# A two-layer token mixer on one core: projections between the score blocks by issue edges, attention weights of the merge in one load

## The chip, the cores and the metric

The kernel runs as one program on one core of a Trainium2 chip. What counts is the device time of one execution in microseconds, as the median over several runs. A NeuronCore has a matmul engine (TensorE, "PE" in the profile, with its weight loads as "PEld"), VectorE ("DVE"), ScalarE ("ACT"), GpSimd ("POOL", unused here) and the queue engine SyncE ("SP"), which issues all large DMAs of this kernel in order.

## The reference, cut to what matters

The model is a two-layer block over 256 context and 256 latent tokens of width 1024. Each layer has a half-step SwiGLU feed-forward network, then three token mixers side by side on one normalised input, then another feed-forward half step. The change is in the mixers and in their merge:

```python
u, gq, gk, gv, nq, nk, nv, gates = split_in(h @ w_in)       # latent; the same of hc for the context
y_ssm = s5_mixer(u, ...)                                     # width 384, with a GLU behind it
y_gqa = window_gqa_latent(rope(gq), rope(gk), gv, ...)       # 8 heads, 2 key/value heads
y_na  = neighborhood_attn_latent(nq, nk, nv, ..., rpb)       # 8 heads
m = sigmoid(g_s) * (y_ssm @ w_p_ssm) + sigmoid(g_a) * (y_gqa @ w_p_gqa) + sigmoid(g_n) * (y_na @ w_p_na)
x = x + ml[5] * (m @ w_out)
```

Latent tokens attend to context and latent, context tokens to the context alone. In the last layer the context has no output, so only its keys, values and recurrence are needed there.

## The kernel before, in words

Activations lie as 128 channels by tokens; columns 0 to 255 are the context, 256 to 511 the latent tokens. Every large product is made of three float32r matmuls (`mm3`): a weight `raw` is loaded by `wload`, ScalarE rounds it to `whi`, VectorE subtracts to get `wlo`, and the product is whi·h + whi·l + wlo·h. `wload` rotates three buffers each of `raw`, `whi` and `wlo` (pool `wp`), and `bank` three PSUM banks.

`mixer(l)` runs once for each layer. `proj(j, a, b)` is one projection of 128 output channels: a load of 512 KB and 24 matmuls of up to 512 columns (256 in layer 1 for what only the latent tokens need, N = 256 there). A loop over `c` handles two head pairs per turn: a GQA attend (heads c and 4 + c) and a neighbourhood attend (NA). Its steps in the order in which they are traced are: GQA queries (`gqa_queries`), one or two gate projections (`fill`), the GQA attend, NA keys and values (`na_keys`), a step of the recurrence (`pump`), NA queries, gates, the NA attend, a step of the recurrence. A gate computed ahead is stored in DRAM (`parked`) and read back in the merge (`gate_back`).

`attend` loops over streams (context and latent; in layer 1 latent alone) and in each over two blocks of 128 queries. A block has four score matmuls into two PSUM banks `sc` (one for each of two heads, hf 0 and 1; there are two such banks), then for each head a softmax on VectorE and ScalarE, transposes on TensorE into `pt` and a copy into `ptb`. A stream ends with `values`, float32 matmuls of 64 weight columns (two passes each) into the two halves of a bank `po`. I write s0b1 for block 1 of the context stream and s1b0 for block 0 of the latent stream.

`put_k` and `put_q` write keys and queries as high and low parts on ScalarE and VectorE; `rotate` applies the rotary angles.

Each engine runs its instructions in the order that is settled when the program is built. The builder goes by what would be ready; among ready instructions of an engine, the one traced first goes first. `tc.issue_after(ins)` queues what is traced inside it, on the engine of `ins`, behind `ins`: an edge of order, not a wait for its end. `pe_anchor[0]` is the last matmul of `mm3` traced so far.

After the loop come three gates (`ths`), the pools of the attention are closed, and the merge opens pool `gp` for `yh` and `yl` (high and low parts of the 11 chunks of y: 3 SSM, 4 GQA, 4 NA) and `mgh`, `mgl`. The SSM output goes through Gelu and the GLU (three banks `pgl`). Then for each of 8 output chunks m the three branches b (SSM 3, GQA 4, NA 4 chunks of k) are multiplied, each with a `wload` of its own weights, gated and added; last the output projection `wout`.

Of the kernel before, what the change touches and what calls it, by code (L numbers as in the profile page):

```python
# [10 lines left out]
F32 = mybir.dt.float32  # L11
# [8 lines left out]
KC = 8  # L20
# [7 lines left out]
def body(tc, A):  # L28
    nc = tc.nc
# [43 lines left out]
    def wload(src, n, pool=None, tag=""):  # L73
        raw = wp.tile([128, 1024], F32, name="raw", tag="raw")
        nc.sync.dma_start(raw[:, :n], src)
        hi = (pool or wp).tile([128, 1024], F32R, name="whi", tag="whi" + tag)
        S.activation(hi[:, :n], raw[:, :n], AF.Copy)  # L77
        lo = (pool or wp).tile([128, 1024], F32R, name="wlo", tag="wlo" + tag)
        anchor[0] = V.tensor_sub(lo[:, :n], raw[:, :n], hi[:, :n].bitcast(F32)).ins  # L79
        return hi, lo  # L80
# [562 lines left out]
    def mixer(l):  # L643
# [89 lines left out]
        def values(nk_, ptb, vt, out):  # L733
            po = pa.tile([128, T], F32, name="po", tag="po")
            for j in range(nk_):
                for hf, r in enumerate(halves):
                    PE.matmul(po[r, :HALF], vt[:, j, r], ptb[hf][:, j], start=j == 0, stop=j == nk_ - 1)  # L737
            S.copy(out, po[:, :HALF])

        def attend(K, Q, vt, out, heads, bias):  # L740

            for s in streams:
                nk_ = 4 if s else 2
                extra = bias() if s else None
                ptb = [ip.tile([128, 4, 2, 128], F32, name="ptb", tag="ptb", bufs=4) for hf in range(2)]
                for b in range(2):
                    q0 = HALF * s + 128 * b
                    ps = [pa.tile([128, T], F32, name="sc", tag="sc", bufs=2) for hf in range(2)]
                    for hf in range(2):
                        for j in range(2):  # L750
                            PE.matmul(ps[hf][:, :128 * nk_], Q[:, hf, q0:q0 + 128], K[:, hf, j, :128 * nk_], start=j == 0, stop=j == 1)  # L751
                    for hf in range(2):
                        if s:
                            k0, n, x = extra(hf, b)
                            V.tensor_add(ps[hf][:, k0:k0 + n], ps[hf][:, k0:k0 + n], x)
                        softmax(ps[hf], nk_, ptb[hf], b, heads[hf], "pt", 1)
                values(nk_, ptb, vt, out[:, HALF * s:HALF * s + HALF])
# [10 lines left out]
        def gqa_queries(c):  # L768
# [5 lines left out]
            return Q  # L774

        def na_keys(c):
            ps = proj(CH_NK + c, 0, T)
            K = stack_k("n")
            put_k(K, slice(0, T), ps)
            return K, v_proj(CH_NV + c, "n")  # L780

# [121 lines left out]
        parked = tc.dram_tile([3 * KC, 128, T], F32, name=f"parked{l}")  # L903
        ahead = [3 * m + b for m in range(1, KC) for b in ((1, 2) if last else (2,))]
        queue = list(ahead)

        def fill():
            for j in queue[:2 if last else 1]:
                queue.remove(j)
                nc.sync.dma_start(parked[j, :, :N], gate(j)[:, :N])  # L910

        def gate_back(j):
            th = mo.tile([128, T], F32, name="th", tag="th", bufs=3)
            nc.sync.dma_start(th[:, :N], parked[j, :, :N])
            return th

        KG = gqa_keys()
        pump()
        for c in range(4):
            Q = gqa_queries(c)  # L920
            fill()
            attend(KG[0], Q, KG[1], gq[:, c], (c, 4 + c), window)
            KN = na_keys(c)
            pump()
            Q = na_queries(c)
            fill()
            attend(KN[0], Q, KN[1], nq[:, c], (None, None), lambda: near(c))
            pump()
        pump(9)
        ths = [gate(j) for j in range(3)]  # L930
        mi.close()

        gp = xs.enter_context(tc.tile_pool(name=f"mg{l}", bufs=1))
        p3 = xs.enter_context(tc.tile_pool(name=f"p3{l}", bufs=3, space=PSUM))
        yh = gp.tile([128, 11, T], F32R, name="yh")
        yl = gp.tile([128, 11, T], F32R, name="yl")
        nat = lambda x: x.rearrange("p (x t) -> p x t", t=8)
# [3 lines left out]
        for c in range(3):  # L941
            split(nat(yh[:, c, c0:]), nat(yl[:, c, c0:]), ty[c])
        pgs = []
        for c in range(3):
            wh, wl = wload(A["wglu"][l, c], 384)
            ps = bank("pgl")
            for k in range(3):
                w = slice(128 * k, 128 * k + 128)
                mm3(ps[:, :N], wh[:, w], wl[:, w], yh[:, k, c0:], yl[:, k, c0:], k == 0, k == 2)
            pgs.append(ps)  # L950
        for c in range(3):
            g = pgs[c][:, :N]
            S.activation(g, g, AF.Tanh, scale=0.5)
            V.scalar_tensor_tensor(ty[c], nat(g), 1.0, ty[c], op0=ALU.add, op1=ALU.mult)
            glu_last = split(nat(yh[:, c, c0:]), nat(yl[:, c, c0:]), ty[c], scale=0.5)
        for src, o in ((gq, 3), (nq, 7)):
            for c in range(4):
                split(yh[:, o + c, c0:], yl[:, o + c, c0:], src[:, c, c0:])
        mh = gp.tile([128, KC, T], F32R, name="mgh")
        ml = gp.tile([128, KC, T], F32R, name="mgl")  # L960
        spans = ((0, 3), (3, 7), (7, 11))
# [15 lines left out]
        for m in range(KC):  # L977
            acc = gp.tile([128, T], F32, name="macc", tag="macc")
            for b, (k0, k1) in enumerate(spans):
                j = 3 * m + b  # L980
                th = ths[b] if m == 0 else gate_back(j) if j in ahead else gate(j)
                wh, wl = wload(A["wp"][l, m][:, 128 * k0:128 * k1], 128 * (k1 - k0))
                pp = p3.tile([128, T], F32, name="pbr", tag="pbr")
                for k in range(k0, k1):
                    w = slice(128 * (k - k0), 128 * (k - k0) + 128)
                    mm3(pp[:, :N], wh[:, w], wl[:, w], yh[:, k, c0:], yl[:, k, c0:], k == k0, k == k1 - 1)
                if b == 0:
                    V.scalar_tensor_tensor(acc[:, :N], th[:, :N], 1.0, pp[:, :N], op0=ALU.add, op1=ALU.mult)
# [3 lines left out]
                if m:  # L992
                    later(0.01 * N + 0.00125 * N * (k1 - k0))
            split(mh[:, m, c0:], ml[:, m, c0:], acc[:, :N])
        later.finish()
# [3 lines left out]
        for s in streams:  # L999
            a, b = HALF * s, HALF * s + HALF  # L1000
            ctx_norm = norm(l, 2, 0, 2) if s and not last else iter(())
            for m in range(KC):
                if m >= 2:
                    next(ctx_norm, None)
                wh, wl = wload(A["wout"][l, m], 1024)
                ps = bank("pwo")
                for k in range(KC):
                    w = slice(128 * k, 128 * k + 128)
                    mm3(ps[:, :HALF], wh[:, w], wl[:, w], mh[:, k, a:b], ml[:, k, a:b], k == 0, k == KC - 1)
                evac_x(m, ps, l, 1, a, b)  # L1010
# [157 lines left out]
```

## Time and profile before

| | |
|---|---|
| median of 3 runs | 2246.77 us (2242.68 to 2249.39) |
| the profiled execution's own time | 2243.03 us |
| span of the profile | 2241.2 us |
| TensorE busy | 2167.7 us, 97% |
| VectorE busy | 1644.6 us, 73% |
| ScalarE busy | 944.7 us, 42% |
| layer 0: attention, merge and output projection from | 484 us, 736 us, 885 us |
| layer 1: the same from | 1736 us, 1930 us, 2005 us |

Times in the profile are microseconds from the span's start. Matmuls overlap: a matmul's duration is longer than its distance to the next, so busy time says little of TensorE's pace. "Idle" before an instruction is the time in which its engine had nothing running, and the name behind the arrow is what ended it.

### The profile page before, as it was taken

How to read it: one execution, taken by the hardware profiler on the slowest of the kernel's cores; microseconds unless marked ns; L12 is line 12 of the kernel's file. 1: busy time of each engine (PE TensorE's matmuls, PEld its weight loads, DVE VectorE, ACT ScalarE, POOL GpSimd, SP SyncE). 2: the span in 40 equal slices, each digit the busy share in tenths (PEclk: the TensorE clock that was granted, in tenths of full speed). 3: DMA queues.
4: the chain of work that ended last, by engine and by line, in shares of the span. 5: the costliest groups of instructions: out<-in, count | busy, mean ns of one | idle time of the engine just before them, and what ended most of it. 6: DMA issues, size and time to landing. Idle time of an engine off the chain costs nothing.

```text
span 2241.2 us, 33869 instructions
## 1 busy us (share of the span) xinstructions
PE 2167.7 (97%) x12842; PEld 1851.8 (83%) x12842; DVE 1644.6 (73%) x3208; ACT 944.7 (42%) x1604; POOL 0.7 (0%) x6
## 2 busy tenths in 40 slices
PE   6999999999999999999999999999999999899997
PEld 3787888987777788988888998888899888798997
DVE  4897887777665888897787797777867776566555
ACT  3322333466566423432222443223245665544443
POOL 0000000000000000000000000000000000000000
PEclk9999999999999999999999999999999999999999
DMA  7635544643431566675565555555556554265554
GB/s 272 210 113 169 198 160 141 224 144 104 137 114 43 176 196 202 207 226 166 183 207 179 165 179 182 162 162 181 179 161 217 160 171 131 70 213 157 172 196 123
DMA packets 141626, 378.16 MB, mean 169 GB/s; under 512 B 30868, under 2 KB 38548, under 8 KB 141464
## 3 DMA queue, kind: packets, MB, share of 16 engines
q1 hardware_dynamic: 140880, 375.88, 52.0%
q8 instruction: 101, 1.65, 0.3%
q14 instruction: 61, 0.50, 0.1%
q10 hardware_dynamic: 584, 0.12, 0.0%
HBM read 346.45 MB, written 29.50 MB: 168 GB/s over the span
## 4 chain that ended last, share of the span: by engine, by line
PE 81%; DVE 9%; ACT 4%; DMA 3%; issue 2%; SPq 0%; ACTq 0%; DVEq 0%
PE pgu L85 11%; PE pgu L83 11%; PE pgu L84 11%; PE pd L85 5%; PE pd L84 5%; PE pd L83 5%; PE pp L83 4%; PE pp L84 4%; PE pp L85 4%; DVE wlo L79 2%; PE po L737 2%; PE pt L729 2%; PE sc L751 2%; ACT whi L77 1%; DMA raw<-dn 1%
## 5 line engine op out<-in xcount | busy, mean ns | idle before, releaser
L77 ACT ACTIVATE whi<-raw 128x1024 fp32r<-128x1024 f32 (+4 forms) x520 | 477.5, 920 | 954.9 <-issue 284.3
L79 DVE TENSOR_TENSOR wlo<-raw,whi 128x1024 fp32r<-128x1024 f32 (+4 forms) x520 | 543.7, 1047 | 281.4 <-ACT whi L77 279.6
L83 PE MATMUL pgu<-Hh,whi 128*128 128x512 f32 (+1 forms) x1360 | 495.1, 365 | 4.2 <-ACT Hh L159 3.0
L85 PE MATMUL pgu<-Hh,wlo 128*128 128x512 f32 (+1 forms) x1360 | 494.7, 364 | 0.9 <-DVE wlo L79 0.9
L84 PE MATMUL pgu<-Hl,whi 128*128 128x512 f32 (+1 forms) x1360 | 494.5, 364 | 0.0
L85 PE MATMUL pd<-mid,wlo 128*128 128x256 f32 (+1 forms) x968 | 305.0, 315 | 2.0 <-DVE wlo L79 2.0
L83 PE MATMUL pd<-mid,whi 128*128 128x256 f32 (+1 forms) x968 | 303.7, 314 | 0.0
L84 PE MATMUL pd<-mid,whi 128*128 128x256 f32 (+1 forms) x968 | 303.4, 313 | 0.0
L83 PEld LDWEIGHTS pgu<-Hh,whi 128*128 128x128 f32 x1360 | 257.9, 190 | 44.9 <-ACT Hh L159 4.0
L85 PEld LDWEIGHTS pgu<-Hh,wlo 128*128 128x128 f32 x1360 | 258.1, 190 | 42.7 <-issue 2.2
L84 PEld LDWEIGHTS pgu<-Hl,whi 128*128 128x128 f32 x1360 | 258.3, 190 | 40.3 <-issue 1.6
L178 DVE SCALAR_TENSOR_TENSOR ajunk<-araw,sb 128x1024 f32<-128x1024 f32 x208 | 255.4, 1228 | 3.4 <-DMA araw<-ada 0.8
L85 PE MATMUL pp<-Hh,wlo 128*128 128x512 f32 (+1 forms) x672 | 238.9, 356 | 3.5 <-DVE wlo L79 3.5
L83 PE MATMUL pp<-Hh,whi 128*128 128x512 f32 (+1 forms) x672 | 239.3, 356 | 0.4 <-ACT th L898 0.4
L84 PE MATMUL pp<-Hl,whi 128*128 128x512 f32 (+1 forms) x672 | 238.2, 354 | 0.0
L85 PEld LDWEIGHTS pd<-mid,wlo 128*128 128x128 f32 x968 | 183.1, 189 | 15.3 <-DVE wlo L79 3.2
L83 PEld LDWEIGHTS pd<-mid,whi 128*128 128x128 f32 x968 | 183.3, 189 | 11.7
L84 PEld LDWEIGHTS pd<-mid,whi 128*128 128x128 f32 x968 | 182.9, 189 | 11.7
L85 PEld LDWEIGHTS pp<-Hh,wlo 128*128 128x128 f32 x672 | 127.6, 190 | 21.8 <-DVE wlo L79 4.7
L83 PEld LDWEIGHTS pp<-Hh,whi 128*128 128x128 f32 x672 | 127.7, 190 | 19.8 <-issue 3.8
L84 PEld LDWEIGHTS pp<-Hl,whi 128*128 128x128 f32 x672 | 127.6, 190 | 17.5 <-issue 3.1
L243 DVE TENSOR_TENSOR gact<-gact,pgu 128x512 f32<-128x512 f32 (+1 forms) x86 | 53.0, 616 | 80.1 <-PE pgu L85 80.0
(298 smaller groups left out, 2884.2 us busy)
## 6 DMA issues: line engine op xcount, KB each, us to landing
raw<-up SPq DMA_DIRECT2D x176, 512.0 KB, 4.0
araw<-ada SPq DMA_DIRECT2D x104, 512.0 KB, 4.0
raw<-win SPq DMA_DIRECT2D x90, 512.0 KB, 3.9
raw<-dn SPq DMA_DIRECT2D x88, 384.0 KB, 3.3
raw<-dn SPq DMA_DIRECT2D x88, 320.0 KB, 3.0
rw<-ada SPq DMA_DIRECT2D x24, 512.0 KB, 3.4
raw<-wout SPq DMA_DIRECT2D x24, 512.0 KB, 4.3
mid<-ada SPq DMA_DIRECT2D x32, 256.0 KB, 4.6
```

Source lines behind the costliest of these rows:

```text
L77: S.activation(hi[:, :n], raw[:, :n], AF.Copy)
L79: anchor[0] = V.tensor_sub(lo[:, :n], raw[:, :n], hi[:, :n].bitcast(F32)).ins
L83: PE.matmul(out, wh, ah, start=first, stop=False)
L84: PE.matmul(out, wh, al, start=False, stop=False)
L85: pe_anchor[0] = PE.matmul(out, wl, ah, start=False, stop=last).ins
L178: V.scalar_tensor_tensor(junk, raw, 1.0, sb[:, s], op0=ALU.mult, op1=ALU.mult, accum_out=mod[:, l, j, s:s + 1])
L243: V.tensor_mul(g[:, :N], g[:, :N], pu[:, :N])
L729: PE.transpose(pt[:, b], p[:, 128 * b:128 * b + 128], ident)
L737: PE.matmul(po[r, :HALF], vt[:, j, r], ptb[hf][:, j], start=j == 0, stop=j == nk_ - 1)
L751: PE.matmul(ps[hf][:, :128 * nk_], Q[:, hf, q0:q0 + 128], K[:, hf, j, :128 * nk_], start=j == 0, stop=j == 1)
```

## The change

The projections of the next step are cut into pieces (keys, values, queries, gates), each with an estimate of its time. `slot()` takes pieces up to some 5 us; `attend` calls it behind the scores of a block (all but the second block of the context stream), with an edge that queues the pieces' matmuls behind these scores; the scores themselves are queued behind the last projection matmul traced. `rest()` traces what is left over. During the GQA attend of turn c the pieces are keys, values and queries of its NA attend; during the NA attend they are the next turn's GQA queries and gates, and in the last turn the three gates `ths`. In layer 1, 11 gates are parked in place of 14. The steps of the recurrence end one turn earlier. `values` writes hf 1 first. In the merge the branches go in the order GQA, NA, SSM; GQA and NA weights come in one load of 1024 columns with buffers of their own (pool `wm`, one set in layer 0, three in layer 1); the splits of both attention outputs are traced ahead of the GLU; `yh`, `yl`, `mgh` and `mgl` are only as wide as the layer needs. In layer 1 every second weight of `wout` uses the `wm` buffers.

```diff
     def wload(src, n, pool=None, tag=""):
-        raw = wp.tile([128, 1024], F32, name="raw", tag="raw")
+        raw = (pool or wp).tile([128, 1024], F32, name="raw", tag="raw" + tag)
...
-                for hf, r in enumerate(halves):
+                for hf, r in ((1, halves[1]), (0, halves[0])):
                     PE.matmul(po[r, :HALF], vt[:, j, r], ptb[hf][:, j], start=j == 0, stop=j == nk_ - 1)
...
-        def attend(K, Q, vt, out, heads, bias):
+        def attend(K, Q, vt, out, heads, bias, slot):
...
-                    for hf in range(2):
-                        for j in range(2):
-                            PE.matmul(ps[hf][:, :128 * nk_], Q[:, hf, q0:q0 + 128], K[:, hf, j, :128 * nk_], start=j == 0, stop=j == 1)
+                    with tc.issue_after(pe_anchor[0]):
+                        for hf in range(2):
+                            for j in range(2):
+                                scored = PE.matmul(ps[hf][:, :128 * nk_], Q[:, hf, q0:q0 + 128], K[:, hf, j, :128 * nk_],
+                                                   start=j == 0, stop=j == 1).ins
+                    if s or b == 0:
+                        with tc.issue_after(scored):
+                            slot()
...
-        ahead = [3 * m + b for m in range(1, KC) for b in ((1, 2) if last else (2,))]
+        ahead = [3 * m + b for m in range(1, KC) for b in ((1, 2) if last and m % 2 else (2,))]
...
+        pieces, got = [], {}
+        whole, part = 5.5, 0.0107 * N
+        def g_pieces(c):
+            return [(part, lambda: got.update(Q=gqa_queries(c)))]
+        def n_pieces(c):
+            def keys():
+                ps = proj(CH_NK + c, 0, T)
+                got["K"] = stack_k("n")
+                put_k(got["K"], slice(0, T), ps)
+            return [(whole, keys), (whole, lambda: got.update(vt=v_proj(CH_NV + c, "n"))),
+                    (part, lambda: got.update(Qn=na_queries(c)))]
+        def slot():
+            us = 0.0
+            while pieces and us < 5.0:
+                t, f = pieces.pop(0)
+                f()
+                us += t
+        def rest():
+            while pieces:
+                pieces.pop(0)[1]()
+        gates = [(part, lambda j=j: park(j)) for j in ahead]
         KG = gqa_keys()
         pump()
+        g_pieces(0)[0][1]()
         for c in range(4):
-            Q = gqa_queries(c)
-            fill()
-            attend(KG[0], Q, KG[1], gq[:, c], (c, 4 + c), window)
-            KN = na_keys(c)
+            pieces += n_pieces(c)
+            attend(KG[0], got["Q"], KG[1], gq[:, c], (c, 4 + c), window, slot)
+            rest()
             pump()
-            Q = na_queries(c)
-            fill()
-            attend(KN[0], Q, KN[1], nq[:, c], (None, None), lambda: near(c))
-            pump()
-        pump(9)
-        ths = [gate(j) for j in range(3)]
+            n = -(-len(gates) // (4 - c))
+            if c < 3:
+                pieces += g_pieces(c + 1)
+            pieces += gates[:n]
+            gates = gates[n:]
+            if c == 3:
+                pieces += [(part, lambda j=j: keep(j)) for j in (1, 2, 0)]
+            attend(got["K"], got["Qn"], got["vt"], nq[:, c], (None, None), lambda: near(c), slot)
+            rest()
+            pump(1 if c < 2 else 4)
...
+        wm = xs.enter_context(tc.tile_pool(name=f"wm{l}", bufs=3 if last else 1))
...
-        yh = gp.tile([128, 11, T], F32R, name="yh")
-        yl = gp.tile([128, 11, T], F32R, name="yl")
+        yh = gp.tile([128, 11, N], F32R, name="yh")
+        yl = gp.tile([128, 11, N], F32R, name="yl")
+        for src, o in ((gq, 3), (nq, 7)):
+            for c in range(4):
+                split(yh[:, o + c], yl[:, o + c], src[:, c, c0:])
...
-            for b, (k0, k1) in enumerate(spans):
+            both = wload(A["wp"][l, m][:, 384:], 1024, wm, "m")
+            for b in (1, 2, 0):
+                k0, k1 = spans[b]
...
-                wh, wl = wload(A["wp"][l, m][:, 128 * k0:128 * k1], 128 * (k1 - k0))
+                wh, wl = both if b else wload(A["wp"][l, m][:, :384], 384)
...
-                if b == 0:
+                if b == 1:
                     V.scalar_tensor_tensor(acc[:, :N], th[:, :N], 1.0, pp[:, :N], op0=ALU.add, op1=ALU.mult)
...
-                wh, wl = wload(A["wout"][l, m], 1024)
+                wh, wl = wload(A["wout"][l, m], 1024, *((wm, "m") if last and m % 2 else ()))
```

## Rows read from the trace of the kernel before

**Rows 1.** The page, section 1: busy time, share of span, instructions by engine.

```profile
PE 2167.7 (97%) x12842; PEld 1851.8 (83%) x12842; DVE 1644.6 (73%) x3208; ACT 944.7 (42%) x1604; POOL 0.7 (0%) x6
```

**Rows 2.** TensorE timeline, two neighbouring projection matmuls: start, us, instruction.

```profile
519.88 0.39 PE L84 MATMUL pp<-Hl,whi 128*128 128x512 f32 x1
520.11 0.39 PE L85 MATMUL pp<-Hh,wlo 128*128 128x512 f32 x1
```

**Rows 3.** Stages: window, us, busy (count) by engine, granted clock, DMA share, GB/s.

```profile
484.00:736.00 252.00, 246.15 (x1330) 184.19 (x1329) 164.54 (x418) 159.44 (x368) 0.00 (x0) 1.00 0.30 98
1736.00:1930.00 194.00, 190.34 (x1253) 162.83 (x1253) 132.26 (x283) 118.88 (x237) 0.00 (x0) 0.97 0.45 138
1930.00:1945.00 15.00, 10.04 (x60) 7.20 (x59) 10.10 (x24) 11.15 (x27) 0.00 (x0) 0.93 0.13 37
1945.00:2005.00 60.00, 55.22 (x429) 53.39 (x427) 37.31 (x75) 26.54 (x45) 0.00 (x0) 0.96 0.62 193
444.30:447.70 3.40, 3.40 (x19) 3.40 (x18) 1.56 (x10) 0.00 (x0) 0.00 (x0) 0.50 0.97 333
```

**Rows 4.** Timeline of TensorE, one values() call and what runs between its two parts.

```profile
507.48 0.65 PE L737 MATMUL po<-ptb,vt 128*64 128x256 f32 x2
508.06 0.88 PE L820 MATMUL pW<-U,WB 128*128 128x64 f32 x6
508.87 1.94 PE L737 MATMUL po<-ptb,vt 128*64 128x256 f32 x14
510.74 0.44 PE L709 MATMUL pvt<-ident,vf 128*128 128x128 f32 x2
```

**Rows 5.** Waits of TensorE, 484 to 736: us in total, times, longest us.

```profile
PE sc L751 <- ACT pr L721: 5.0, 5, 1.5
```

**Rows 6.** Timeline of TensorE, scores of the context and latent blocks in layer 0.

```profile
524.01 0.40 PE L751 MATMUL sc<-K,Q 128*128 128x256 f32 x2
...
524.48 0.40 PE L751 MATMUL sc<-K,Q 128*128 128x256 f32 x2
...
526.68 0.67 PE L751 MATMUL sc<-K,Q 128*128 128x512 f32 x2
...
527.85 0.62 PE L751 MATMUL sc<-K,Q 128*128 128x512 f32 x2
...
545.48 0.64 PE L751 MATMUL sc<-K,Q 128*128 128x256 f32 x4
...
549.76 0.39 PE L751 MATMUL sc<-K,Q 128*128 128x256 f32 x1 [1.12 <-ACT pr L721]
```

**Rows 7.** Groups by form, 484 to 736: busy us, mean ns, idle, releaser.

```profile
L721 ACT ACTIVATE pr<-sc,st 128x256 f32<-128x256 f32 x32 | 15.2, 477 | 1.9 <-DVE st L719 1.3 <-DVE st L717 0.5
...
L692 DVE TENSOR_TENSOR K<-pp,K 64x512 fp32r<-64x512 f32 x8 | 5.5, 687 | 1.3 <-ACT K L691 1.2
...
L690 ACT ACTIVATE K<-pp 64x512 fp32r<-64x512 f32 x8 | 4.7, 591 | 0.5 <-DVE K L693 0.4
```

**Rows 8.** Waits of TensorE, 1736 to 1930.

```profile
PE sc L751 <- DVE Q L685: 1.5, 2, 0.8
```

**Rows 9.** The page, section 6: DMA issues, count, KB each, us to landing.

```profile
raw<-win SPq DMA_DIRECT2D x90, 512.0 KB, 3.9
```

**Rows 10.** Waits of TensorE, 736 to 885.

```profile
PE pbr L83 <- ACT yh L88: 1.6, 2, 0.9
PE pbr L84 <- DVE yl L92: 1.2, 2, 1.0
```

**Rows 11.** Waits of TensorE, 1930 to 1945.

```profile
PE pbr L83 <- ACT whi L77: 2.4, 2, 2.1
...
PE pgl L83 <- ACT yh L88: 1.0, 1, 1.0
```

**Rows 12.** Waits of TensorE, 1945 to 2005.

```profile
PE pp L85 <- DVE wlo L79: 3.5, 6, 1.6
```

**Rows 13.** Timeline of TensorE, the sum of a norm ahead of layer 0's mixer.

```profile
443.42 0.58 PE L115 MATMUL nps<-ones,nacc 128*128 128x1 f32 x4 [1.74 <-DVE zp L845]
```

More of the change, by code (lines that the diff above doesn't have):

```diff
@@ L774, in gqa_queries @@
             return Q
[L776 to L780, printed above, removed]
         def na_queries(c):
@@ L903, in mixer, with park, keep @@
         parked = tc.dram_tile([3 * KC, 128, T], F32, name=f"parked{l}")
-        ahead = [3 * m + b for m in range(1, KC) for b in ((1, 2) if last else (2,))]
[L905 to L910, printed above, removed]
+        ahead = [3 * m + b for m in range(1, KC) for b in ((1, 2) if last and m % 2 else (2,))]
+        ths = {}
+        def park(j):
+            nc.sync.dma_start(parked[j, :, :N], gate(j)[:, :N])
+        def keep(j):
+            ths[j] = gate(j)
         def gate_back(j):
@@ L941, in mixer @@
         for c in range(3):
-            split(nat(yh[:, c, c0:]), nat(yl[:, c, c0:]), ty[c])
+            split(nat(yh[:, c]), nat(yl[:, c]), ty[c])
         pgs = []
@@ L948, in mixer @@
                 w = slice(128 * k, 128 * k + 128)
-                mm3(ps[:, :N], wh[:, w], wl[:, w], yh[:, k, c0:], yl[:, k, c0:], k == 0, k == 2)
+                mm3(ps[:, :N], wh[:, w], wl[:, w], yh[:, k], yl[:, k], k == 0, k == 2)
             pgs.append(ps)
@@ L954, in mixer @@
             V.scalar_tensor_tensor(ty[c], nat(g), 1.0, ty[c], op0=ALU.add, op1=ALU.mult)
[L955 to L960, printed above, removed]
+            glu_last = split(nat(yh[:, c]), nat(yl[:, c]), ty[c], scale=0.5)
+        mh = gp.tile([128, KC, N], F32R, name="mgh")
+        ml = gp.tile([128, KC, N], F32R, name="mgl")
         spans = ((0, 3), (3, 7), (7, 11))
@@ L978, in mixer @@
             acc = gp.tile([128, T], F32, name="macc", tag="macc")
-            for b, (k0, k1) in enumerate(spans):
+            both = wload(A["wp"][l, m][:, 384:], 1024, wm, "m")
+            for b in (1, 2, 0):
+                k0, k1 = spans[b]
                 j = 3 * m + b
                 th = ths[b] if m == 0 else gate_back(j) if j in ahead else gate(j)
-                wh, wl = wload(A["wp"][l, m][:, 128 * k0:128 * k1], 128 * (k1 - k0))
+                wh, wl = both if b else wload(A["wp"][l, m][:, :384], 384)
+                w0 = 3 if b else 0
                 pp = p3.tile([128, T], F32, name="pbr", tag="pbr")
                 for k in range(k0, k1):
-                    w = slice(128 * (k - k0), 128 * (k - k0) + 128)
-                    mm3(pp[:, :N], wh[:, w], wl[:, w], yh[:, k, c0:], yl[:, k, c0:], k == k0, k == k1 - 1)
-                if b == 0:
+                    w = slice(128 * (k - w0), 128 * (k - w0) + 128)
+                    mm3(pp[:, :N], wh[:, w], wl[:, w], yh[:, k], yl[:, k], k == k0, k == k1 - 1)
+                if b == 1:
                     V.scalar_tensor_tensor(acc[:, :N], th[:, :N], 1.0, pp[:, :N], op0=ALU.add, op1=ALU.mult)
@@ L993, in mixer @@
                     later(0.01 * N + 0.00125 * N * (k1 - k0))
-            split(mh[:, m, c0:], ml[:, m, c0:], acc[:, :N])
+            split(mh[:, m], ml[:, m], acc[:, :N])
         later.finish()
@@ L1008, in mixer @@
                     w = slice(128 * k, 128 * k + 128)
-                    mm3(ps[:, :HALF], wh[:, w], wl[:, w], mh[:, k, a:b], ml[:, k, a:b], k == 0, k == KC - 1)
+                    mm3(ps[:, :HALF], wh[:, w], wl[:, w], mh[:, k, a - c0:b - c0], ml[:, k, a - c0:b - c0], k == 0, k == KC - 1)
                 evac_x(m, ps, l, 1, a, b)
```

## The prediction

> **What bounds the kernel now.** I read the page first. TensorE is busy for 97% of the span [rows 1], so only time taken away from TensorE, or idle time of it, can change the end. But "busy" hides the real pace: in an undisturbed run of projection matmuls each row lasts 0.39 us while the starts are 0.23 us apart [rows 2], so a projection of 24 matmuls costs 24 x 0.227 = 5.45 us at 512 columns, about 2.75 us at 256. I judge everything below by spacing from start to start, not by duration. Then I cut the span into the stages that the change touches [rows 3]: layer 0's attention has 5.9 us of idle TensorE in 252, layer 1's 3.7 in 194, the passage to layer 1's merge 5.0 in 15, and that merge 4.8 in 60 (its clock 0.96). The pool to be won is some tens of us, no more. The projections of the next step are already mixed into the score blocks matmul by matmul; the change orders this mixture anew.
>
> **Values in one group.** Each `values()` call writes two column halves of one bank. Today hf 0's first matmul is issued as soon as its half of `ptb` is there, alone; the other matmuls follow later in one run [rows 4]. The lone one is two passes and holds TensorE for 508.06 - 507.48 = 0.58 us; the other 14 passes take 510.74 - 508.87 = 1.87 us, 0.13 each, because the halves run beside each other, though the last two passes have no partner either. That hf 0's second matmul did not run early with the first shows that the writes to the bank keep their order. So with hf 1 first, which is ready last, nothing can start early, both halves run side by side from the first pass to the last, and 16 passes should take what 14 do now. There are 24 calls (8 attends of two streams, 8 of one), and 23 show this lone pair: 23 x 0.58 = 13.3 us gained, with re-entry about 0.1 each not counted. Bounds: 0 (the group is split all the same) and 15.6.
>
> **Layer 0: the edges.** Now TensorE idles there before score blocks: 5.0 us for the Exp that must free the two score banks, in 5 places [rows 5]. With the overlap that each stop loses (0.39 - 0.23 = 0.16), 5 x 0.16 + 5.0 = 5.8 us. After the change a piece of 24 matmuls is traced right behind a block's scores, ahead of that block's softmax, so it goes first: 5.45 us pass between these scores and the next, the Exp is long done, and the 5.8 us go away.
>
> But the edges make a new wait. In the context stream the second block has no slot (`if s or b == 0`), and the first block of the latent stream comes straight behind it: scores s0b1, then scores s1b0, then the next piece. s1b0 writes the banks that s0b1's Exp must free; the piece's 24 matmuls are queued behind s1b0's scores, and nothing else may pass but transposes. What this takes, [rows 6] show. Where little stood in the way, the first half's scores of the latent block came 526.68 - 524.01 = 2.67 us behind the context block's, the second half's 527.85 - 524.48 = 3.37. Between the two context blocks of a GQA attend, where the `put_q` of a projection that had just ended stood ahead on ScalarE and VectorE, it was 549.76 - 545.48 = 4.28. From the start of s0b1 to the next piece it is thus 0.23 + 3.37 + 0.45 = 4.1 us up to 4.28 + 0.45 + some 0.8 for the second Exp = 5.5, in which TensorE has 0.46 of scores, 0.2 of transposes and 0.9 of scores: idle 2.5 to 4.0 us. In the new order the piece before is K or the next Q. K's `put_k` alone puts 4 x 0.59 us on ScalarE and 4 x 0.69 on VectorE ahead of an Exp of 0.48 [rows 7]. That is nearer to the upper case; I take 3.3. This comes 7 times (4 attends behind K, 3 behind a Q); the eighth stands behind a gate, with one Tanh, 1 us. Sum: 7 x 3.3 + 1 = 24 us lost; bounds 18 and 30. Before, TensorE had projections of lower rank to fill just this time.
>
> **Layer 1: the edges.** Only one stream runs, every block has a slot, and no such pair exists. Of the 3.7 us of idle time [rows 3], 1.5 are waits for Q [rows 8]; these stay, since the queries are projected right ahead of their scores in `rest()`, with only the recurrence's matmuls as cover. The other 2.2, for Exp, transposed weights and a gate, are covered by the pieces: 2.2 us gained, bounds 4 gained and 2 lost. Three gates fewer are parked: their 24 matmuls move to the merge, at the same price, 0; three stores and three loads of 128 KB vanish, which lay beside matmuls.
>
> **DMAs and the queue.** Each moved projection takes its load of 512 KB along on SP; it is issued ahead of the bias load of the same attend, which is wanted only behind a piece of 5.45 us. I cost this at 0; without the cover it would be one landing, 3.9 us each [rows 9].
>
> **The merge.** In layer 0 TensorE waits 2.8 us for the gated SSM result [rows 10]. Now the two attention branches come first and cover it, but their splits and the new buffers for `both` lie in memory that the attention pools give back at its end, so the load of 512 KB, cast and subtraction follow only then. I take 1.5 gained. In layer 1 the same passage has waits of 2.4 for weights and 1.0 for `yh` [rows 11]; by the same reasoning 2 gained. Bounds for both together: 6 gained, 2 lost. In layer 1's merge TensorE waits 3.5 us for the subtraction of gate weights [rows 12]; three buffers more and one load for two branches should take most of it, and with it some of the 1.3 us that a cast keeps it waiting and some clock (0.96 [rows 3]): 5 gained, bounds 0 and 9. In layer 0's merge the single `both` buffer is free when branch 2's matmuls end; branch 0 and the next gate (7.5 us and 5.45) lie between that and its next use, so 0; were the cover gone, a landing and two conversions, about 4 + 2 us per output chunk, would show. The output projection's alternating buffers: 0.5.
>
> **Sum.** -13.3 - 5.8 + 24 - 2.2 - 3.5 - 5 - 0.5 = -6.3 us. The profiled execution took 2243.0 (span 2241.2 and 1.8 around it), so 2236.7 on its scale. The median of the runs shown is 3.7 higher, which would be 2240.4; some 0.1 us for each of the 23 re-entries were left out, so I forecast 2238.
>
> **Rivals.** (1) *The new waits in layer 0 cost clock too* (slower). In this trace a wait of 1.74 us up to 443.42 [rows 13] is followed by 3.4 us at granted clock 0.50, the 1.2 GHz level [rows 3]; the waits before Exp, at most 1.5 us [rows 5], were followed by none. The new ones, at 2.5 to 4, are longer than both. One such stretch costs 3.4 / 2 = 1.7 us; eight cost 14, and with waits of 4.0 (another 5) the time is 2238 + 19 = 2257. It tells as slower from about six such stretches of the eight. The Trainium skill, "TensorE: Matmul & The Clock Gate", section "HAM oscillation — how this bites in real kernels", says that idle gaps between bursts of matmuls bring the clock back to half rate again and again; by it I would add the 14 us, and the row at 443.42 agrees with it; against it stands that the idle time here is broken by short scores. Chance 0.25. (2) *The waits are hidden*: recurrence matmuls, transposes and late values fall into them, or the softmax gets ahead of `put_k`. Then most of the 24 us are not lost: 2238 - 20 = 2218; with the merge's upper bound 2210. For it: matmuls of the recurrence do fill such places now (pW in [rows 4]); against: in the new order they are queued at the head of an attend and should be done by then. Chance 0.25. (3) *Values are still split*, so the change does not do what it says there: 2238 + 13 = 2251. The order in [rows 4] speaks against it; chance 0.08. (4) My forecast, 0.42.
>
> **From this the numbers.** Forecast 2238; within it the terms' bounds give about +-9. The range that leaves out no more than 2 in 10 runs from 2212 (most of rival 2) to 2258 (rival 1); the likeliest case alone has 2229 to 2247. A measurement tells about 0.3%, 6.7 us, from no change: faster means below 2240.0, slower above 2253.5. My own case lies close to the first line: of its 0.42 I give 0.25 to faster and 0.17 to the same. Rival 2 is all faster, rival 1 0.2 slower and 0.05 the same, rival 3 half and half. Faster 0.5, same 0.26, slower 0.24.
>
> **What would show it.** Values: rows of 16 passes (8 in the context stream), 1.9 us from start to next, no lone pair. Edges: in layer 0 runs of 24 unbroken projection matmuls, then idle before the scores of s1b0 ended by Exp, eight times, 2.5 to 4 us; the waits for Exp elsewhere gone. Rival 1 would show as stretches at 0.50 behind these waits. Merge: the branch of the attention first behind the GLU matmuls, less waiting for `wlo` in layer 1. Wrong I would be if the waits of s1b0 are not there or fill up, if the clock falls at most of them, or if the merge waits longer for its first `both` load than it waited for the SSM branch.

## The result, and the profile after

The changed kernel takes 2276.67 us (median of 4 runs, 2270.4 to 2277.33) against 2244.93 of the kernel before on the same chip (4 runs, 2242.68 to 2249.39). The ratio is 1.0134, 95% interval 1.0122 to 1.0146: slower by about 30 us, outside the predicted range. The profiled execution took 2270.4 us, with a span of 2268.6, 27.4 longer than that of before.

TensorE's busy time in the page of the changed kernel is the same as in [rows 1]:

```profile
PE 2167.7 (96%) x12842; PEld 1858.2 (82%) x12842; DVE 1650.8 (73%) x3192; ACT 942.4 (42%) x1588; POOL 0.7 (0%) x6
```

What differs is where it stands still and at which clock. The stages of the changed kernel, in the columns of [rows 3]: layer 0's attention, layer 1's, and layer 1's merge (from the first matmul of the GLU). The last two lines are short stretches that come back below, the idle one up to 556.30 and the one behind it, at 0.50, the 1.2 GHz level:

```profile
478.20:767.80 289.60, 254.43 (x1352) 192.85 (x1352) 170.12 (x423) 161.57 (x374) 0.00 (x0) 0.97 0.28 90
1761.70:1968.30 206.60, 197.49 (x1257) 169.56 (x1257) 136.98 (x292) 123.09 (x249) 0.00 (x0) 0.92 0.39 124
1968.30:2033.60 65.30, 64.71 (x534) 63.97 (x533) 50.15 (x82) 35.96 (x56) 0.00 (x0) 1.00 0.74 245
...
552.30:556.30 4.00, 0.67 (x7) 0.47 (x5) 3.96 (x8) 3.69 (x7) 0.00 (x0) 1.00 0.00 0
557.95:561.36 3.41, 3.41 (x9) 2.67 (x10) 3.25 (x12) 1.21 (x3) 0.00 (x0) 0.50 0.65 196
```

Layer 0's attention has 289.6 - 254.4 = 35.2 us of idle TensorE, where [rows 3] have 5.9. Layer 1's merge has almost none left. The waits of TensorE in layer 0's attention (us in total, times, longest), where the kernel before had the 5.0 us of [rows 5] and one of 0.7 us for the first queries:

```profile
PE pt L729 <- ACT ptb L730: 22.3, 12, 3.3
PE sc L753 <- DVE Q L685: 6.0, 6, 4.2
PE pvt L709 <- ACT vf L706: 4.8, 4, 1.4
PE sc L753 <- ACT pr L721: 2.5, 7, 0.5
```

In layer 1 (just ahead of the attention, then in it) the counterpart of [rows 8] is:

```profile
PE sc L753 <- DVE Q L685: 7.3, 1, 7.3
...
PE pt L729 <- ACT ptb L730: 3.9, 5, 1.0
...
PE pt L729 <- ACT Q L684: 1.4, 1, 1.4
```

And all that TensorE waits for in layer 1's merge, against [rows 12]:

```profile
PE pbr L85 <- DVE wlo L79: 0.3, 1, 0.3
PE pbr L84 <- DVE yl L92: 0.2, 1, 0.2
```

One of the new waits, from the timeline of the changed kernel (start, us, engine; weight loads and DMA issues left out):

```profile
551.88 0.39 PE L85 MATMUL pp<-Hh,wlo 128*128 128x512 f32 x1
...
552.08 1.06 ACT L77 ACTIVATE whi<-raw 128x1024 fp32r<-128x1024 f32 x1 [2.09 <-PE pp L84]
552.11 0.38 PE L729 MATMUL pt<-ident,pr 128*128 128x128 f32 x2
...
552.25 0.72 PE L753 MATMUL sc<-K,Q 128*128 128x256 f32 x4
...
553.39 0.62 ACT L835 COPY sw<-z 64x512 f32<-64x512 f32 x1 [0.24 <-DVE z L833]
...
554.01 0.62 ACT L836 COPY sw<-z 64x512 f32<-64x512 f32 x1
...
554.65 0.59 ACT L690 ACTIVATE K<-pp 64x512 fp32r<-64x512 f32 x1
...
555.26 0.59 ACT L691 ACTIVATE K<-pp 64x512 fp32r<-64x512 f32 x1
...
555.87 0.37 ACT L730 COPY ptb<-pt 128x256 f32<-128x256 f32 x1
556.14 0.48 ACT L721 ACTIVATE pr<-sc,st 128x256 f32<-128x256 f32 x1
...
556.30 0.44 PE L729 MATMUL pt<-ident,pr 128*128 128x128 f32 x2 [3.33 <-ACT ptb L730]
...
556.76 0.50 PE L753 MATMUL sc<-K,Q 128*128 128x512 f32 x1
...
557.85 1.15 PE L753 MATMUL sc<-K,Q 128*128 128x512 f32 x2 [0.35 <-ACT pr L721]
```

The piece ends at 552. Only then come the transposes of s0b0's first head and the scores of s0b1, since the piece was traced ahead of the softmax. The second head's transposes need the one bank `pt`, which ScalarE copies out only after a weight's cast, two copies of the recurrence and two conversions of K; the Exp of s0b1, which frees banks for s1b0's scores, stands right behind. TensorE is idle for 3.33 + 0.35 = 3.7 us. This is the place that the prediction named (s0b1 to s1b0, eight times). In the eight attends the idle time there is 2.1, 2.1, 3.7, 2.2, 3.7, 2.2, 2.1 and 1.2: 19.2 us before rounding.

Two other kinds of place were not foreseen. The transposes of V wait for the copy of V's own projection, four times, and at the end of each GQA attend the second head's transposes, then the next scores, wait 1.4 and 0.4 us:

```profile
500.21 0.66 PE L709 MATMUL pvt<-ident,vf 128*128 128x128 f32 x4 [1.38 <-ACT vf L706]
...
510.83 0.66 PE L729 MATMUL pt<-ident,pr 128*128 128x128 f32 x4 [1.43 <-ACT ptb L730]
...
511.85 0.50 PE L753 MATMUL sc<-K,Q 128*128 128x256 f32 x2 [0.37 <-DVE Q L685]
512.29 1.95 PE L737 MATMUL po<-ptb,vt 128*64 128x256 f32 x16
514.16 2.00 PE L820 MATMUL pW<-U,WB 128*128 128x64 f32 x16
```

The last two lines answer to [rows 4]: 16 passes in one run take 514.16 - 512.29 = 1.87 us, as 14 did before, and no lone pair is left.

By the starts of the first GLU matmul and the first output-projection matmul in both traces, and with the measured 0.58 us for each lone pair, the 27.4 us come about so (what "measured" gives for the values is a count of pairs, not a time taken in this trace):

| term | forecast | measured | how |
|---|---|---|---|
| values in one group | -13.3 | -13.4 | 16 + 7 pairs of 0.58 |
| mixer's order, layer 0 | +18.2 | +40.8 | GLU starts at 767.85, before 736.38; 9.3 of values added back |
| mixer's order, layer 1 | -2.2 | +15.6 | GLU at 1968.30, before 1936.43; three gates (8.2), values (4.1) and layer 0's merge (2.9) added back, 31.5 taken off |
| merge, layer 0 | -1.5 | -2.9 | 145.5 us, before 148.5 |
| merge, layer 1 | -7.0 | -11.3 | 65.3 us, before 68.3, with 8.2 of gates more in it |
| behind it | -0.5 | -1.4 | the rest |

The 40.8 us are rather too few: the profiled execution of before lost 3.4 us ahead of layer 0's attention, in two stretches of 3.4 us at 0.50 (from 417.0, and from 444.3 [rows 3]), that of the changed kernel none before its wait for the first queries.

### The profile page after: what moved, and what is told of

Its sections match the earlier page's. It is cut to its first block, busy times and chain, and to the rows that moved or that the text cites. A ratio compares the mean times of both kernels' runs of the same rounds, so it can differ in the third digit from the quotient of the medians.

```text
span 2268.6 us, 33757 instructions
## 1 busy us (share of the span) xinstructions
PE 2167.7 (96%) x12842; PEld 1858.2 (82%) x12842; DVE 1650.8 (73%) x3192; ACT 942.4 (42%) x1588; POOL 0.7 (0%) x6
## 5 line engine op out<-in xcount | busy, mean ns | idle before, releaser
L77 ACT ACTIVATE whi<-raw 128x1024 fp32r<-128x1024 f32 (+2 forms) x504 | 474.5, 943 | 996.1 <-issue 326.2
L79 DVE TENSOR_TENSOR wlo<-raw,whi 128x1024 fp32r<-128x1024 f32 (+2 forms) x504 | 541.8, 1077 | 306.5 <-ACT whi L77 295.7
```

## The experiments

Each was timed in 3 rounds beside the kernel before; I give the ratio to it with its 95% interval. Differences between two such runs are those of their medians; by the ratios some come out otherwise, 60 us in place of 64 for e6 below. The theory at the start: the mixer's order loses, values and merge gain. Its rivals stand with each run.

### The parts by themselves

**e1_values**: the kernel before with the order of halves in `values` alone.

```diff
-                for hf, r in enumerate(halves):
+                for hf, r in ((1, halves[1]), (0, halves[0])):
```

> The kernel before with hf 1 written first in values, and nothing else. If the lone pair of passes is all that changes, the 23 lone pairs of 0.58 us go and 16 passes take 1.88 us in one run: 13.3 us less, a ratio of 0.994. Rival: the group starts later, waits for the second head's copy and gives the time back as idle time: 0 to 5 us less.

2229.07 us, ratio 0.9935 (0.9913 to 0.9956): 12.0 below before, as expected. But not in the expected places, so the agreement of the total is in part luck. By the first GLU matmul of layer 0 it is 17.9 us ahead (718.47, before 736.38): 13.3 from the attention's first scores on, where 16 pairs make 9.3, and 4.6 ahead of them, 3.4 of it the two half-clock stretches of before, which are missing here. Layer 1's attention, where 4.1 of the pairs' time lay, takes 201.6 us, before 200.2. There the granted clock is 0.94, where [rows 3] have 0.97:

```profile
1721.80:1923.40 201.60, 195.27 (x1277) 168.14 (x1277) 133.94 (x285) 122.05 (x246) 0.00 (x0) 0.94 0.44 136
```

**e2_best_parts**: that and the merge of the change (all of the diff below `mi.close()`, and `wload`), with before's mixer.

> The kernel before, its mixer untouched but for the order in values, with the whole merge part of the change (one load for both attention branches, own buffers, order GQA, NA, SSM, early splits, narrow yh and mgh); 14 gates parked as before. If the mixer's edges alone lose and the other parts keep what the trace after shows (13.3 for values, 2.9 for layer 0's passage to the merge, 11.3 for layer 1's merge, 1.4 behind it), it takes about 29 us less than before, near 2216. Rival: the merge gains because the edges left TensorE and the queue in another state at the end of the attention; then only values and part of the merge stay, 13 to 20 us less.

2213.85 us, ratio 0.9868 (0.9846 to 0.9890): 27 below before, 15 of it by the merge. In layer 1's merge, where [rows 12] had 3.5 us, the wait for `wlo` is 0.8.

**e3_mixer_only**: the changed kernel with `values`, `wload` and the merge of before.

> The changed kernel with values and the merge as before, so the new order of the mixer alone. If the parts add up, 2276 + 13 + 15 = about 2304 us, a ratio of 1.026 to before. Rival: the parts hide each other's waits, and it stays below 2290.

2296.39 us, ratio 1.0234 (1.0206 to 1.0262). Between the two figures: the order of the mixer costs some 55 us by itself, and the other parts bring 20 on top of it, where they bring 27 on the old mixer. Layer 1's attention has clock 0.98 here, with `values` in two parts as before:

```profile
1783.40:1980.70 197.30, 190.24 (x1256) 161.29 (x1257) 132.97 (x283) 120.08 (x241) 0.00 (x0) 0.98 0.42 128
```

### Which edge

**e4_no_edges**, **e5_no_edge_scores** and **e6_no_edge_pieces** take away both edges, the first line below alone, or the second alone:

```diff
-                    with tc.issue_after(pe_anchor[0]):
+                    if True:
                         for hf in range(2):
...
-                        with tc.issue_after(scored):
-                            slot()
+                        slot()
```

> The changed kernel without both edges of order in attend (the scores are not queued behind the last projection, the pieces not behind the scores); the order of tracing stays. If the edges make the waits, TensorE fills them again with projections as before, and with the gains of values and merge the time comes to 2216 to 2230 us. Rival: it is the order of tracing, the pieces standing ahead of the softmax's transposes, that delays the softmax; then most waits stay, and it is at 2260 or above.

2208.99 us, ratio 0.9844 (0.9817 to 0.9870): the edges, not the order of tracing, and 7 us below the lower figure.

> The changed kernel without the edge that queues the scores behind the last projection traced; the pieces stay queued behind the scores. Theory: TensorE stands still only where both edges meet (scores that may not go earlier, a piece that may not go before them). With free scores the blocks' softmax starts inside the piece ahead, and most waits go: 2205 to 2230 us. Rival: the edge of the pieces alone makes the waits, since nothing but transposes may be done until the scores are out: 2255 or above.

2277.04 us, ratio 1.0157 (1.0133 to 1.0180): nothing gained. The theory of the two edges together falls, its rival holds.

> The changed kernel without the edge that queues the pieces behind the scores; the scores stay queued behind the last projection traced ahead of them. Theory: the next piece may now fill the time in which the latent block's scores wait, so most waits go: 2205 to 2235 us. Rival: the edge of the scores alone makes the waits (each block's softmax starts only after a whole piece): 2255 or above.

2212.28 us, ratio 0.9866 (0.9843 to 0.9888). One line, the edge that queues the pieces behind the scores, makes 64 us of difference; the order of tracing stays as it was. Its stages (layer 0's and layer 1's attention) and all its waits in layer 0:

```profile
479.80:725.40 245.60, 239.59 (x1337) 181.67 (x1337) 166.31 (x423) 160.38 (x374) 0.00 (x0) 1.00 0.33 106
1722.70:1915.00 192.30, 188.22 (x1225) 164.29 (x1226) 133.92 (x290) 121.00 (x248) 0.00 (x0) 0.92 0.43 133
```

```profile
PE pt L729 <- DVE pr L726: 1.7, 4, 0.6
PE sc L753 <- ACT pr L721: 1.2, 4, 0.5
PE sc L753 <- DVE Q L685: 0.8, 1, 0.8
PE pt L729 <- ACT ptb L730: 0.2, 1, 0.2
```

Idle time is 6.0 us again in place of 35.2, and the 22.3 us of waits for `ptb` are gone, though ScalarE does the same work. The timeline of TensorE shows what stands there now: projection matmuls around each pair of the latent block's scores.

```profile
547.11 0.39 PE L85 MATMUL pp<-Hh,wlo 128*128 128x512 f32 x1
548.00 0.73 PE L753 MATMUL sc<-K,Q 128*128 128x512 f32 x2 [0.50 <-ACT pr L721]
548.57 0.39 PE L83 MATMUL pp<-Hh,whi 128*128 128x512 f32 x1
...
550.23 0.50 PE L753 MATMUL sc<-K,Q 128*128 128x512 f32 x1
550.56 0.38 PE L729 MATMUL pt<-ident,pr 128*128 128x128 f32 x2
550.70 0.48 PE L753 MATMUL sc<-K,Q 128*128 128x512 f32 x1
551.01 0.40 PE L84 MATMUL pp<-Hl,whi 128*128 128x512 f32 x1
```

**e12_edge_layer1**: the pieces' edge in layer 1 alone (`if last:` around it).

> The changed kernel with the edge of the pieces in layer 1 alone; the edge of the scores stays in both. Layer 0's attention took 289.7 us with both edges and 245.6 without that of the pieces, layer 1's 206.6 and 192.2. If the loss sits mainly in layer 0, where two streams share the banks, it is 2276 - 44 = 2230 to 2236. Rival: layer 1, with small work of the recurrence alone as cover, costs as much: 2245 or above.

2229.31 us, ratio 0.9941 (0.9922 to 0.9961). So the edge costs 2276.7 - 2229.3 = 47 us in layer 0 and 2229.3 - 2212.3 = 17 in layer 1.

### Where pieces are put

**e7_slot_all**: `if True:` in place of `if s or b == 0:`, so that s0b1 has a slot.

> The changed kernel with a slot behind every block, the second of the context stream too; both edges stay. In layer 0 the stretches from the scores of s0b1 to the next piece lose 27 us in the trace after (19.4 of it idle) and 6.8 us of clock behind them. If the missing slot is their cause, 20 to 30 us come back: 2246 to 2256. Rival: a wait follows the edges to another block, since three pieces now stand for four slots: 0 to 10 us back, 2266 or above.

2291.20 us, ratio 1.0215 (1.0195 to 1.0235): slower than the change itself by 14 us. The waits in layer 0's attention:

```profile
PE sc L753 <- ACT pr L721: 20.5, 12, 3.3
PE pt L729 <- ACT ptb L730: 7.4, 11, 1.1
PE pvt L709 <- ACT vf L706: 6.5, 4, 1.9
```

The waits for `ptb` shrink from 22.3 to 7.4 us, but three pieces for four slots leave another block bare: now scores wait for an Exp, 20.5 us. The missing slot only decided where the wait falls.

**e8_gate_first**: gates ahead of the first attend, as before.

```diff
         g_pieces(0)[0][1]()
+        for _ in range(2 if last else 1):
+            gates.pop(0)[1]()
         for c in range(4):
```

> The changed kernel with one parked gate (layer 1: two) projected ahead of the first attend, as the kernel before has it; all else stays. In the trace after TensorE waits 4.4 us (layer 0) and 7.5 us (layer 1) more than its pace for the first queries. If the gate covers this, 8 to 12 us come back: 2264 to 2268. Rival: the wait only moves to the end of the last attend, which now has a piece less: under 3 us back.

2270.61 us, ratio 1.0134 (1.0103 to 1.0164): the ratio of the change itself, though the median is 6 us lower, so 0 to 6 us came back, and neither expectation is settled. In layer 1 two waits for an Exp took the place of most of the wait for the first queries; they stand in the middle of the attention (at 1860.9 and 1915.5), not at the end of the last attend, as the rival had it.

```profile
PE sc L753 <- ACT pr L721: 4.0, 2, 2.0
PE sc L753 <- DVE Q L685: 2.6, 3, 1.5
```

**e10_slot_late**: `slot` traced behind the softmax of its block, both edges kept.

```diff
-                    if s or b == 0:
-                        with tc.issue_after(scored):
-                            slot()
                     for hf in range(2):
...
                         softmax(ps[hf], nk_, ptb[hf], b, heads[hf], "pt", 1)
+                    if s or b == 0:
+                        with tc.issue_after(scored):
+                            slot()
```

> The changed kernel with slot traced behind the softmax of its block, both edges kept; transposes now rank ahead of the piece's matmuls. If the waits are made by the piece going ahead of the softmax's transposes, most of them go: 2220 to 2240 us. Rival: with the edge kept, nothing may fill while scores wait, whatever ranks first: 2262 or above.

2256.44 us, ratio 1.0066 (1.0043 to 1.0089): 20 us come back, 44 against e6 do not. Neither figure was met: the order of tracing sets how long the waits are, the edge that they are there. Its waits in layer 0:

```profile
PE sc L753 <- ACT pr L721: 16.2, 8, 2.6
PE sc L753 <- DVE Q L685: 6.8, 4, 4.2
```

These eight waits, 1.2 to 2.6 us, all at s1b0's scores and all for the Exp, are those that the prediction described.

**e15_no_edges_late**: the same without both edges.

> The changed kernel without both edges, and with slot traced behind the softmax of its block. With the edges kept this order of tracing brought 20 us. If the order matters by itself, it brings some here too: 2195 to 2205 against the 2209 without edges. Rival: without the edge of the pieces TensorE finds other work whichever ranks first: 2205 to 2215.

2211.60 us, ratio 0.9861 (0.9846 to 0.9875): the rival. Without the edge the order of tracing makes no difference that can be measured.

### What sets the length of the waits

**e9_joint_pt**: in the context stream the second head's transposes go into the free half of the first head's `pt` bank.

```diff
-            pt = pa.tile([128, 4, 128], F32, name="pt", tag=tag, bufs=bufs)
+            if nk_ == 2 and joint:
+                pt, o = joint[0], 2
...
-                PE.transpose(pt[:, b], p[:, 128 * b:128 * b + 128], ident)
+                PE.transpose(pt[:, o + b], p[:, 128 * b:128 * b + 128], ident)
```

> The changed kernel with the transposes of both heads of a context block in one pt bank (they fit: 2 x 2 x 128 columns), so the second head's no longer wait for the first head's copy to ptb. In the trace after most of the idle time between the scores of s0b1 and the next piece ends with that copy, not with the Exp that the prediction named. If the bank makes the waits, 15 to 20 us come back in layer 0: 2257 to 2262. Rival: the Exp of s0b1, which stands in the same queue of ScalarE behind the conversions of K, ends hardly earlier; the wait only changes its name: under 5 us back, 2271 or above.

2275.62 us, ratio 1.0149 (1.0125 to 1.0173). Inconclusive: the transposes still waited for the first head's copy, 22.3 us in 12 places, so the wait that was to go was not taken away.

**e13_joint_pt_copies_last**: the same, and both copies traced behind both heads' transposes.

```diff
+            if keep:
+                return pt
-            S.copy(ptb[:, :nk_, c], pt[:, :nk_])
+            S.copy(ptb[:, :nk_, c], pt[:, o:o + nk_])
+            if pt_in:
+                S.copy(first[:, :nk_, c], pt[:, :nk_])
```

> The changed kernel; in the context stream both heads' transposes go into one pt bank, and both copies to ptb stand behind them, so no transpose waits for a copy. In the run with the joint bank alone the same wait of 22.3 us remained, since the copy was still ahead of the second head's transposes. If the pt bank makes the waits, 15 to 20 us come back: 2257 to 2262. Rival: the waiting is for ScalarE's queue (cast of a weight, the recurrence's copies, K's conversions, which stand ahead of copy and Exp alike), and the Exp of s0b1 takes the copy's place: under 5 us back, 2271 or above.

2289.14 us, ratio 1.0209 (1.0192 to 1.0226), 12 more than the change. Some 9 of the 12 are clock: layer 0's attention takes 304.3 us at 0.94, where the change has 0.97. In layer 0:

```profile
PE sc L758 <- ACT pr L721: 22.2, 9, 3.9
...
PE pt L730 <- ACT ptb L733: 5.7, 4, 1.4
```

The bank is cleared of it: without its wait, the wait for the Exp is as long, up to 3.9 us. Both stand behind the same work in ScalarE's queue.

**e14_putk_late**: `put_k` as a piece of its own, of no time, so that it is traced behind the softmax of s0b1.

> The changed kernel with K's conversions (put_k) traced in the next slot, behind the softmax of s0b1, in place of ahead of it. The prediction named them as what holds up the Exp. In the trace after two of them (1.2 us) stand ahead of the copy and the Exp in each of the four GQA attends. If they lengthen the waits, 4 x 1.2 = 5 us and some clock come back: 2266 to 2272. Rival: the cast and the recurrence's copies ahead of them, or V's conversions behind, take their place: 2274 or above.

2269.03 us, ratio 1.0117 (1.0102 to 1.0132). The idle time at s0b1 in the four GQA attends falls from 2.1 and 3.7 us to 1.4 and 2.2, and the waits for `ptb` in layer 0 from 22.3 to 17.4, with 2.2 the longest. So K's conversions are part of what is waited for, as the prediction had it. Whether the time falls can't be told: the intervals touch, and the profiled execution lost more clock in this stage (0.95 of 290.2 us) than the change (0.97).

### The clock

**e11_dummy**: six matmuls behind s0b1's scores, into one of the three banks that `bank` rotates.

```diff
+                    else:
+                        with tc.issue_after(scored):
+                            ps_ = bank("dm")
+                            for k in range(6):
+                                PE.matmul(ps_, Hh[:, 0, :128], Hh[:, k], start=k == 0, stop=k == 5)
```

> The changed kernel with six matmuls of 512 columns more (no use is made of their result) behind the scores of s0b1, in the time in which TensorE stands idle there: 1.36 us in each of the 8 places, which waits of 1.2 to 3.7 us cover. The time of the waits stays. If the half clock behind four of these waits comes from the idle time, the stretches at granted clock 0.50 behind 556, 599, 631 and 674 us go, at 1.7 us each: 5 to 8 us less, 2269 to 2272. Rival: the clock falls all the same (or the six cost time): 2275 to 2285.

2273.77 us, ratio 1.0141 (1.0117 to 1.0164): no change in time that can be told. In the trace two of the four stretches at 0.50 are gone, those behind the two waits of 2.2 us (599 and 674); one stayed, one lies elsewhere. Layer 0's attention has clock 0.98 in place of 0.97:

```profile
482.80:771.20 288.40, 262.29 (x1400) 198.92 (x1400) 169.59 (x423) 161.66 (x374) 0.00 (x0) 0.98 0.29 90
```

So work in the waits keeps some of the clock; what it gives back, at most 3.4 us, is below what can be measured here.

### The version to keep

**e16_no_edges_gate**: e4 with the gates of e8 ahead of the first attend.

> The changed kernel without both edges, and with one parked gate (layer 1: two) ahead of the first attend. Without edges the first scores still wait 0.8 and 0.9 us for their queries. If the gate covers it and nothing else moves, 2206 to 2209. Rival: the last attend, with one piece less, waits longer: 2209 to 2214.

2212.18 us, ratio 0.9862 (0.9847 to 0.9877), in the range of its rival. e4, e6, e15, e16 and e2 lie within each other's intervals: 27 to 32 us below before, some 64 below the change. What they share is `values` and the merge, and that projections are free to fill any gap. A gain of the new trace order over before's is not shown.

## Why the prediction was wrong

- **Values**: right in mechanism. No lone pair and 1.87 us for 16 passes; rival 3 falls. The sum of -12.0 us alone is near the 13.3 in part by luck (e1). That layer 1's share is lost again with its clock (e1) was not foreseen.
- **Layer 0, the waits removed**: half right. The waits for an Exp went from 5.0 to 2.5 us, not to nothing.
- **Layer 0, the edges**: this is the step that failed. It looked for a block without a slot and costed one wait per attend: "the piece's 24 matmuls are queued behind s1b0's scores, and nothing else may pass but transposes". The place was right and the size nearly so (idle 1.2 to 3.7 us, forecast 1 to 4.0; 19.2 us in all, forecast 24, and 6.8 us of clock behind four of them). But the rule that it found there holds at every block: behind the edge no projection may start until the scores before it are out, so whatever those scores or transposes wait for is bare. That gave 5 us at V's transposes, 4 x 1.8 at the ends of the GQA attends, and 4.6 at the first queries. Had each place in which TensorE waits for small work been gone through with the question "what may fill it now", the sum would have had the other sign. e6 shows the cause, e7 that another slot does not help.
- **What the wait is for**: the reason given, ScalarE's queue with K's conversions ahead of the Exp, holds (e13, e14), with the recurrence's copies and a cast ahead of it as well. That the transposes of the block before would come only after the piece was missed; it is worth 20 us (e10).
- **Layer 1, the edges**: failed with the same thought. "Every block has a slot, and no such pair exists" gave -2.2; it is +15.6 by the traces (some 6 us of it clock that goes with the order of `values`, 0.03 of 200), and e12 gives 17 for the edge. The first queries alone make TensorE wait 7.3 us, where before's gates covered all but 0.8 [rows 8]; the prediction said that these waits stay, and did not see that the gates ahead of the first attend, their cover, had been moved into slots. Without the edge the wait is 0.9 us, with the gates where the change has them (e6).
- **Rival 1, clock**: right as a mechanism, too small as a sum. Behind the four longest waits (3.7 and 2.2 us, twice each) a stretch of 3.4 us at 0.50 follows, 1.7 us each, and a stretch of 6.8 us lies at the first queries; behind the other four waits at s0b1 there is none. By the Trainium skill, "TensorE: Matmul & The Clock Gate", section "HAM oscillation — how this bites in real kernels", idle gaps between bursts bring the clock down again and again; the trace agrees in four of eight places. In layer 1 the granted clock is 0.92 with the edge and without (e6), so there the edge is not its cause.
- **Rival 2, waits hidden**: wrong here, but it is what happens without the edge (2212; it said 2218).
- **Merge**: right in sign, larger than forecast: -11.3 in place of -7 in layer 1, -2.9 in place of -1.5 in layer 0; together with what lies behind it 15.6, and 15 as the difference of e2 and e1. TensorE's waits in layer 1's merge are 0.5 us where [rows 12] alone had 3.5, and the clock is 1.00 where [rows 3] had 0.93 and 0.96.
- **DMAs and the queue**: no wait for a load shows in either attention; 0 was right.

TensorE does not choose: the Trainium skill, "PSUM — Partial Sum Buffer", section "Engine vs sequencer instructions", says that matmuls start and complete in program order. The trace agrees in the wait at 552: the next projection's weights, counted back through the three buffers, were rounded from 533.98 and subtracted by 536.31, and its matmuls stood behind scores that were not ready until 557.85.

## What to carry to other kernels

Here an edge of order on the work that fills gaps took away the cover of every wait behind it on that engine, not only of the one in view: before adding one, list every wait on its far side and say what may still run there. Leave low-rank filler free, and use the order of tracing for preference; here the same order cost nothing that can be told without the edge, and 60 to 64 us with it. When one part of a change is suspected, run the others without it: values and merge together were worth 27 us that the edge hid.

## What the runs showed that was not expected

In layer 1's attention the granted clock went with the order of `values`: 0.97 in the kernel before and 0.98 in e3, which write the halves in two parts; 0.94 in e1, where nothing else is changed, and 0.92 in the changed kernel and in e6, which write them in one run, as do the thirteen other kernels here, with 0.91 to 0.95. The 4.1 us saved there are lost again. In layer 0's attention the clock stays at 1.00 in e6 with the same order. What in layer 1 makes the difference stays open: no run here separates it, and each clock is that of one profiled execution.

In layer 0 the length of a wait alone does not tell whether half clock follows. In the changed kernel waits of 2.2 us were followed by 3.4 us at 0.50 in both their places, and waits of 2.1 us in none of three; with 1.36 us of matmuls in the gap (e11) both stretches were gone. But of e11's two waits of 1.93 + 0.35 us the one up to 562.47 was followed by such a stretch and the one up to 636.81 was not, and in e14 a wait of 2.12 us up to 556.97 came with 6.8 us at 0.50:

```profile
556.90:563.70 6.80, 6.61 (x17) 4.65 (x18) 5.94 (x17) 3.01 (x11) 0.00 (x0) 0.50 0.47 154
```

What decides it stays open.
